# The recurrent layer of a decoder trunk: order of its blocks, form of its gates and gelu, and its first loads

## The chip, the cores and the metric

The kernel runs on one core of a Trainium2 chip. The metric is the device time in microseconds of one execution. The engines are TensorE (PE; PEld is its weight load), VectorE (DVE), ScalarE (ACT), GpSimd (POOL) and SyncE (SP, which issues most DMAs).

## The reference

One recurrent layer is followed by one attention layer, each with a SwiGLU part; 512 tokens, width 1024. The change is in the recurrent layer's mixer alone:

```
proj = rms_norm(x) @ w_in                  # 1024 -> 2048, split in y (first half) and x (second half)
gate = gelu(y, approximate=True)           # tanh form
xc   = causal_depthwise_conv(x)            # 4 taps per channel
r, i = sigmoid(xc @ w_a + b_a), sigmoid(xc @ w_x + b_x)     # 8 diagonal blocks of 128 x 128
log_a = -8 * r * softplus(-lambda);  a = exp(log_a)
u = sqrt(-expm1(2 * log_a)) * i * xc
h_t = a_t * h_(t-1) + u_t                  # scan over the tokens
x = x + (gate * h) @ w_out
```

All inputs and outputs are float32.

## The kernel before

Activations lie transposed: a tile is 128 channels by 512 tokens, the residual stream is eight such tiles `h[0..7]`. A float32 product is made of three matmuls (`mm3`, lines 132 to 136): both operands are split into a rounded high part (`xh`, `wh`) and the rest (`xl`, `wl`), and high*high, high*low and low*high are summed in one PSUM bank. A weight piece is 128 x 1024, one block of 128 output channels; with eight k steps of three matmuls a block takes 24 matmuls of 512 columns.

`Stream` (lines 64 to 125) brings the pieces in order: a DMA on SP's queue into one of two raw buffers (`wr`), then the split: ACT makes `wh` (line 92), and DVE subtracts for `wl` (line 99), or, for pieces of the kind "dma", ACT writes the negated high part (line 95) and a DMA on GpSimd's queue adds the weight to it (line 96). `wh` and `wl` have three buffers each. `get(i)` loads two pieces ahead and splits one ahead. The tile framework orders each engine's instructions from program order, priorities and its own time model, and sets the semaphores.

The start: SP issues the parameters, then the x tiles with the first two weight pieces between them (each in two halves). The split of x makes `xh[k]` on ACT and `xl[k]` on DVE with the norm's gain; the row factor of the norm is multiplied in afterwards, when a block leaves PSUM. The first two blocks run side by side over k (lines 274 to 279). The squares of x (ACT, line 217) are added up on DVE (line 218); `norm_factors` sums over partitions by small matmuls (line 226) and takes the inverse root on DVE; `norm_rows` spreads it with one float32 matmul (line 239), and ACT copies it into `rb` (line 241).

The layer then runs 16 blocks in `lru_order`: five x blocks, then y and x in turn, then the last y blocks. `x_block` (328 to 341) multiplies PSUM by `rb` on DVE, convolves (one ACT, three DVE instructions) and splits the result. `x_gates` (343 to 361) makes two `mm3` products with the split gate weights, in banks "S" (one buffer) and "PT" (two), then two sigmoids and a tanh on ACT. `load_gates` (322 to 326) brings the gate weights on ACT's queue, through the raw buffers `wr`, and splits them. `recur(half)` (363 to 387), once for four blocks, makes exp, square and sqrt on ACT and the scan on DVE. `y_block` (392 to 401) makes the gelu of a square, a tanh (both ACT) and two DVE products; `y_gate` (403 to 405) multiplies with the scanned value and splits into `hgh`, `hgl`. `act_order` orders the groups of ACT functions by edges that make no semaphore. `out_proj` (244 to 256) then runs eight output blocks of 24 matmuls one after the other, and the first SwiGLU part follows. Banks for blocks: four of the tag "mm".

Of the kernel before, what the change touches and what calls it, by code (L numbers as in the profile page):

```python
# [48 lines left out]

class Pool:  # L50
# [13 lines left out]
class Stream:  # L64


    def __init__(self, tc, nc, pool, pieces, ahead_load, ahead_split):
        self.tc, self.nc, self.pool, self.pieces = tc, nc, pool, pieces
        self.al, self.asp = ahead_load, ahead_split
        self.raw, self.parts = {}, {}  # L70
        self.nl = self.ns = self.halved = 0

    def _load(self, i):
# [4 lines left out]
        return [lambda c=c: self.nc.sync.dma_start(r[:, c], ap[:, c]) for c in self._cuts(i, w)]  # L78

    def _cuts(self, i, w):  # L80
        return [slice(0, 512), slice(512, 1024)] if i < self.halved else [slice(0, w)]

    def _split(self, i):
# [6 lines left out]
        def do(c):  # L90
            with self.tc.high_priority():
# [11 lines left out]
    def start(self, n):  # L103

        self.halved = self.nl = self.ns = n
        loads, splits = zip(*[(self._load(i), self._split(i)) for i in range(n)])
        return [[x[j] for x in y] for y in (loads, splits) for j in range(2)]
# [20 lines left out]
def trunk(tc, A, out):  # L128
# [17 lines left out]
    lru_order = [8, 9, 10, 11, 12, 0, 13, 1, 14, 2, 15, 3, 4, 5, 6, 7]  # L146
# [15 lines left out]
    with tc.tile_pool(name="keep", bufs=1) as kp, tc.tile_pool(name="wts", bufs=3) as wp, \  # L162
# [24 lines left out]
        G.memset(ones, 1.0)  # L187
# [16 lines left out]
        def split(src, gain, hi, lo):  # L204
            S.activation(hi, src, AF.Copy, scale=gain)  # L205
            V.scalar_tensor_tensor(lo, src, gain, hi.bitcast(F32), ALU.mult, ALU.subtract)  # L206

# [4 lines left out]
        def squares(k, pool, tag="sq", bufs=1):  # L212
            if k == 0:
                S.activation(ssum, h[0], AF.Square)
            else:
                sq = pool.tile([128, T], F32, name="sq", tag=tag, bufs=bufs)
                S.activation(sq, h[k], AF.Square)
                V.tensor_add(ssum, ssum, sq)
# [15 lines left out]
        def norm_rows(pool, r, tag="sq", bufs=1):  # L234
            dg = pool.tile([128, T], F32, name="dg", tag=tag, bufs=bufs)
            ps = bank("O")
            for n in range(4):
                V.tensor_scalar(dg[:, 128 * n:128 * n + 128], ident, r[:, n:n + 1], None, ALU.mult)
            PE.matmul(ps, ones, dg, start=True, stop=True)
            rb = pool.tile([128, T], F32, name="rb", bufs=1)  # L240
            S.copy(rb, ps)
# [17 lines left out]
        with tc.tile_pool(name="lru", bufs=2) as lp, \  # L259
                tc.tile_pool(name="few", bufs=2) as ls:  # L260
            lp = Pool(lp)
            small = Pool(ls)
            for k in range(KB):
                split(h[k], gain(C_AN, k), xh[k], xl[k])
                run(split_a if k == 0 else split_b if k == 3 else ())
            def in_block(i):
                ps = bank()
                wh, wl = ws.get(i)
                for k in range(KB):
                    c = slice(128 * k, 128 * k + 128)  # L270
                    mm3(ps, (wh[:, c], wl[:, c]), (xh[k], xl[k]), k == 0, k == KB - 1)
                return ps
# [15 lines left out]
            sp8, nsp8 = (small.tile([128, 8], F32, name=n, bufs=1) for n in ("sp8", "nsp8"))  # L288
# [14 lines left out]
            V.tensor_scalar(sp8, lam, -1.0, 0.0, ALU.mult, ALU.max)  # L303
            V.scalar_tensor_tensor(sp8, l3, 2.0, sp8, ALU.mult, ALU.add)
            V.tensor_scalar(sp8, sp8, 8.0, None, ALU.mult)
            V.tensor_scalar(nsp8, sp8, -1.0, None, ALU.mult)
# [7 lines left out]
            gw = [lp.tile([128, 1024], F32R, name=f"gw{i}", bufs=1) for i in range(4)]  # L314
            gated, rate, tau, last_act = [None] * 8, [None] * 4, [None] * 4, [None]

            def act_order(inst):

                tc.add_manual_dep(inst.ins, last_act[0].ins.name, mybir.DependencyInfo(
                    mybir.DependencyClass.NoSync, mybir.DependencyReason.DATA), reason="table order")  # L320

            def load_gates():
                for g in range(2):
# [626 lines left out]
```

## Time and profile before

| | us |
|---|---|
| median of 3 runs | 1257.73 |
| lowest and highest run | 1252.86 and 1258.27 |
| the profiled execution's own time | 1258.03 |
| its span (first to last instruction) | 1256.3 |
| PE, PEld busy | 1222.4 (97%), 1014.8 (81%) |
| DVE, ACT busy | 680.5 (54%), 550.1 (44%) |

A matmul's record is longer than the distance to the next one, since matmuls are pipelined; what one costs is read from the distance between starts. The clock that was granted to TensorE stands in the tables of stretches as a share of 2.4 GHz. The page cuts the span in 40 slices: PE is busy for 7 tenths of the first, 8 of the second and 8 of the fifth, and for 9 tenths or more of nearly all the others.

### The profile page before, as it was taken

What the parts mean: (1) busy time and instruction counts of PE and PEld (TensorE: products, weight loads), DVE (VectorE), ACT (ScalarE), POOL (GpSimd) and SP (SyncE); (2) the same over time, 40 slices, a digit from 0 to 9 for tenths busy, and PEclk for the clock granted to TensorE, in tenths of its full rate; (3) what the DMA queues carried; (4) which work ended last, traced back from release to release, by engine and by line L of the source; (5) the groups of instructions that cost most, each with busy time, mean ns of one, the idle gap of its engine ahead of it and who ended that gap; (6) DMA issues with size and microseconds to landing.
All of it is one profiled execution on the core that took longest, in us unless ns stands there. A gap on an engine that the chain in (4) does not pass through costs nothing.

```text
span 1256.3 us, 14918 instructions
## 1 busy us (share of the span) xinstructions
PE 1222.4 (97%) x5634; PEld 1014.8 (81%) x5634; DVE 680.5 (54%) x1356; ACT 550.1 (44%) x996; POOL 101.9 (8%) x108
## 2 busy tenths in 40 slices
PE   7899899999999999999999999999999999999998
PEld 6678688888888888887878888898888888888887
DVE  7778855444554333377446665765745544552221
ACT  5799533223332222365576766555522323232210
POOL 0100001011111000010111100000011111110000
PEclk9899999999999999999999998599999999999999
DMA  5554222322232333332888664024332233323331
GB/s 190 130 134 118 84 98 87 101 101 93 92 101 97 93 92 95 110 112 86 201 178 186 137 134 101 1 49 99 105 96 91 99 101 101 99 84 103 121 118 46
DMA packets 41257, 133.98 MB, mean 107 GB/s; under 512 B 4960, under 2 KB 7136, under 8 KB 41184
## 3 DMA queue, kind: packets, MB, share of 16 engines
q1 hardware_dynamic: 34416, 110.17, 27.6%
q0 software_dynamic: 5760, 20.97, 10.0%
q10 hardware_dynamic: 1008, 1.88, 0.5%
q8 instruction: 44, 0.72, 0.2%
q14 instruction: 29, 0.24, 0.1%
HBM read 129.86 MB, written 2.10 MB: 105 GB/s over the span
## 4 chain that ended last, share of the span: by engine, by line
PE 79%; ACT 8%; DVE 8%; DMA 3%; issue 1%; SPq 0%; DVEq 0%; ACTq 0%
PE ps L135 23%; PE ps L136 23%; PE ps L134 23%; PE ps L641 3%; PE ps L642 3%; PE ps L643 3%; ACT junk L583 2%; DMA wr<-in_w_q 2%; ACT wh L92 1%; DVE kn L600 1%; ACT wl L95 1%; PE ps L716 1%; DVE wl L99 1%; PE ps L786 1%; DVE gated L386 1%
## 5 line engine op out<-in xcount | busy, mean ns | idle before, releaser
L92 ACT CAST wh<-wr 128x1024 fp32r<-128x1024 f32 (+2 forms) x206 | 210.7, 1024 | 478.7 <-PE ps L135 443.3
L134 PE MATMUL ps<-xh,wh 128*128 128x512 f32 x896 | 353.6, 395 | 11.7 <-ACT xh L205 6.0
L135 PE MATMUL ps<-xl,wh 128*128 128x512 f32 x896 | 351.0, 392 | 0.3 <-DVE xl L206 0.3
L136 PE MATMUL ps<-xh,wl 128*128 128x512 f32 x896 | 351.1, 392 | 0.0
L99 DVE TENSOR_TENSOR wl<-wr,wh 128x1024 fp32r<-128x1024 f32 (+2 forms) x166 | 238.9, 1440 | 152.4 <-ACT wh L92 152.3
L134 PEld LDWEIGHTS ps<-xh,wh 128*128 128x128 f32 x896 | 169.5, 189 | 48.2 <-ACT xh L205 5.9
L135 PEld LDWEIGHTS ps<-xl,wh 128*128 128x128 f32 x896 | 169.6, 189 | 35.9 <-DVE xl L206 1.0
L136 PEld LDWEIGHTS ps<-xh,wl 128*128 128x128 f32 x896 | 169.5, 189 | 35.7 <-issue 0.2
L134 PE MATMUL ps<-gh,wh 128*128 128x512 f32 x352 | 136.9, 389 | 0.0
L135 PE MATMUL ps<-gl,wh 128*128 128x512 f32 x352 | 136.9, 389 | 0.0
L136 PE MATMUL ps<-gh,wl 128*128 128x512 f32 x352 | 136.9, 389 | 0.0
L450 DVE TENSOR_TENSOR u<-ps,rb 128x512 f32<-128x512 f32 x44 | 30.4, 691 | 139.2 <-PE ps L136 139.2
L451 POOL TENSOR_TENSOR u<-u,g 128x512 f32<-128x512 f32 x44 | 59.6, 1354 | 506.7 <-ACT wh L92 362.9
L641 PE MATMUL ps<-wh,xh 128*128 128x512 f32 x224 | 91.2, 407 | 0.0
L643 PE MATMUL ps<-wh,xl 128*128 128x512 f32 x224 | 87.7, 392 | 0.0
L642 PE MATMUL ps<-wl,xh 128*128 128x512 f32 x224 | 87.4, 390 | 0.0
L136 PEld LDWEIGHTS ps<-gh,wl 128*128 128x128 f32 x352 | 66.1, 188 | 13.8
L134 PEld LDWEIGHTS ps<-gh,wh 128*128 128x128 f32 x352 | 66.1, 188 | 13.7
L135 PEld LDWEIGHTS ps<-gl,wh 128*128 128x128 f32 x352 | 66.1, 188 | 13.6
L448 DVE TENSOR_TENSOR g<-ps,rb 128x512 f32<-128x512 f32 x44 | 30.4, 691 | 63.0 <-PE ps L136 62.7
L209 ACT CAST gh<-u 128x512 fp32r<-128x512 f32 x44 | 27.3, 621 | 62.0 <-POOL u L451 62.0
L95 ACT ACTIVATE wl<-wr 128x1024 fp32r<-128x1024 f32 x40 | 42.2, 1056 | 19.0 <-PE ps L642 12.3
(208 smaller groups left out, 1533.8 us busy)
## 6 DMA issues: line engine op xcount, KB each, us to landing
wr<-in_f_in SPq DMA_DIRECT2D x88, 512.0 KB, 3.4
wr<-in_f_out SPq DMA_DIRECT2D x32, 512.0 KB, 3.5
wr<-in_w_q SPq DMA_DIRECT2D x24, 512.0 KB, 6.4
wl<-in_w_q POOLq DMA_DIRECT2D x24, 512.0 KB, 7.0
wr<-in_w_in SPq DMA_DIRECT2D x14, 512.0 KB, 3.7
wr<-in_f_out SPq DMA_DIRECT2D x16, 384.0 KB, 3.1
wr<-in_w_kv SPq DMA_DIRECT2D x12, 512.0 KB, 3.5
wl<-in_w_in POOLq DMA_DIRECT2D x8, 512.0 KB, 7.3
```

Source lines behind the costliest of these rows:

```text
L92: nc.scalar.copy(hi[:, c], r[:, c])
L95: nc.scalar.mul(lo[:, c], r[:, c], -1.0)
L99: eng.tensor_tensor(lo[:, c], r[:, c], hi[:, c].bitcast(F32), ALU.subtract)
L134: PE.matmul(ps, wh, xh, start=first, stop=False)
L135: PE.matmul(ps, wh, xl, start=False, stop=False)
L136: PE.matmul(ps, wl, xh, start=False, stop=last)
L448: V.tensor_tensor(g, pair[0], rb, ALU.mult)
L450: V.tensor_tensor(u, pair[1], rb, ALU.mult)
L451: G.tensor_tensor(u, u, g, ALU.mult)
L641: PE.matmul(ps[t], xh[k][:, r], wh[:, c], start=k == 0, stop=False)
L642: PE.matmul(ps[t], xh[k][:, r], wl[:, c], start=False, stop=False)
L643: PE.matmul(ps[t], xl[k][:, r], wh[:, c], start=False, stop=k == 7)
```

## The change

It does the following in the recurrent layer. The x blocks come first and the y blocks after them. The gate products are single float32 matmuls on unsplit `xc` and unsplit gate weights, which SP loads after the first two blocks straight into their own tiles. The gelu is one ACT function; sqrt works on a tanh of half the argument, so that the square is gone; ACT's functions are ordered in runs. The first two pieces are cut in three, with the first two cuts on ACT's queue; eleven bfloat16 matmuls on a constant tile stand at the start. The norm's small matmuls stand inside the third block and `norm_rows` inside the fourth, with `rb` copied by DVE; a fifth block runs before `rb` is used, in a "PT" bank. The subtractions for piece 3 and 4 are ordered behind the last sum of squares and the last `dg`. Weights are split two ahead in the block loop. The first two output blocks run side by side.

```diff
     def _load(self, i):
-        return [lambda c=c: self.nc.sync.dma_start(r[:, c], ap[:, c]) for c in self._cuts(i, w)]
+        return [lambda c=c, q=q: q.dma_start(r[:, c], ap[:, c]) for c, q in
+                itertools.zip_longest(self._cuts(i, w), self.queues if i < self.cut else (), fillvalue=self.nc.sync)]
...
-        return [slice(0, 512), slice(512, 1024)] if i < self.halved else [slice(0, w)]
+        return [slice(0, 256), slice(256, 512), slice(512, 1024)] if i < self.cut else [slice(0, w)]
...
-                    eng.tensor_tensor(lo[:, c], r[:, c], hi[:, c].bitcast(F32), ALU.subtract)
+                    a = eng.tensor_tensor(lo[:, c], r[:, c], hi[:, c].bitcast(F32), ALU.subtract)
+                    if i in self.hold:
+                        behind(self.tc, a, self.hold[i])
...
-    lru_order = [8, 9, 10, 11, 12, 0, 13, 1, 14, 2, 15, 3, 4, 5, 6, 7]
+    lru_order = [8, 9, 10, 11, 12, 13, 14, 15, 0, 1, 2, 3, 4, 5, 6, 7]
...
-        load_a, load_b, split_a, split_b = ws.start(2)
+        load_a, load_b, load_c, *splits = ws.start(2, nc.scalar, nc.scalar)
         nc.sync.dma_start(par, A["par"])
+        run(load_a + load_b)
         for k in range(KB):
             nc.sync.dma_start(h[k], A["x"][k])
-            run(load_a if k == 0 else load_b if k == 2 else ())
+            run(load_c if k == 3 else ())
...
+            warm = lp.tile([128, T], F32, name="warm", tag="y", bufs=4).bitcast(BF16)[:, :T]
+            V.memset(warm, 1.0)
+            idle = bank("S")
+            for _ in range(11):
+                PE.matmul(idle, warm[:, 0:128], warm, start=True, stop=True)
             for k in range(KB):
-                split(h[k], gain(C_AN, k), xh[k], xl[k])
-                run(split_a if k == 0 else split_b if k == 3 else ())
+                with tc.high_priority():
+                    a = split(h[k], gain(C_AN, k), xh[k], xl[k])
+                    if k:
+                        behind(tc, a, before)
+                    before = a
+                run(splits.pop(0) if k in (0, 1, 3) else ())
...
-            for k in range(KB):
-                squares(k, lp, "q", 2)
-            first.append(in_block(2))
-            r = norm_factors(small)
-            rb = norm_rows(lp, r, "q", 2)
+            gw = [lp.tile([128, 1024], F32, name=f"gw{i}", bufs=1) for i in range(2)]
+            for g in range(2):
+                nc.sync.dma_start(gw[g], A["gates"][g])
+            with tc.high_priority():
+                for k in range(KB):
+                    ws.hold[3] = squares(k, lp, "q", 3)
+            norm = []
+            def soon(fn, *args):
+                with tc.high_priority():
+                    norm.append(fn(*args))
+            first.append(in_block(2, between=lambda: soon(norm_factors, small)))
+            first.append(in_block(3, between=lambda: soon(norm_rows, lp, norm[0], "q", 3, V.tensor_copy, 4)))
+            rb = norm[1]
+            first.append(in_block(4, "PT"))
...
-                ch = lp.tile([128, T], F32R, name="ch")
-                cl = lp.tile([128, T], F32R, name="cl")
-                halve(xc, ch, cl)
-                return b, xc, ch, cl
+                return b, xc
...
-                mm3(pr, (gw[0][:, c], gw[1][:, c]), (ch, cl), True, True)
-                mm3(pi, (gw[2][:, c], gw[3][:, c]), (ch, cl), True, True)
+                PE.matmul(pr, gw[0][:, c], xc, start=True, stop=True)
+                PE.matmul(pi, gw[1][:, c], xc, start=True, stop=True)
...
+            def decays(half):
+                end_run()
+                for b in range(4 * half, 4 * half + 4):
+                    a = rate[b // 2][:, T * (b % 2):T * (b % 2) + T]
+                    done.append(S.activation(a, a, AF.Exp, scale=nsp8[:, b:b + 1]))
+                    act_order(done[-1])
+                end_run()
+                for t in tau[2 * half:2 * half + 2]:
+                    done.append(S.activation(t, t, AF.Sqrt))
+                    act_order(done[-1])
+                end_run()
+            def recur(b):
+                a, t = (x[b // 2][:, T * (b % 2):T * (b % 2) + T] for x in (rate, tau))
+                V.scalar_tensor_tensor(gated[b], a, 1.0, gated[b], ALU.add, ALU.mult)
+                V.tensor_tensor(gated[b], gated[b], t, ALU.mult)
+                V.tensor_tensor_scan(gated[b], a, gated[b], 0.0, ALU.mult, ALU.add)
...
-                t = lp.tile([128, T], F32, name="t", bufs=3)
-                S.activation(t, y, AF.Square, scale=math.sqrt(0.044715))
-                V.scalar_tensor_tensor(t, t, 1.0, y, ALU.add, ALU.mult)
-                S.activation(t, t, AF.Tanh, scale=math.sqrt(2.0 / math.pi))
-                V.scalar_tensor_tensor(t, t, 1.0, y, ALU.add, ALU.mult)
-                return b, t
+                return b, y
+            def y_gate(b, y):
+                g = S.activation(y, y, AF.Gelu_apprx_tanh)
+                act_order(g)
+                V.tensor_tensor(mine(y), mine(y), perm(gated[b]), ALU.mult)
+                halve(y, hgh[b], hgl[b])
...
+            ws.asp = 2
...
-                while xs and xs[0][0] + 2 <= i:
-                    st = xs.pop(0)[1]
-                    x_gates(*st)
-                    if st[0] % 4 == 3:
-                        recur(halves)
-                        halves += 1
-                while ys and ys[0][0] < 4 * halves:
+                for b in decayed[:2]:
+                    recur(decayed.pop(0))
+                while xs and xs[0][0] + (3 if xs[0][0] < 5 else 2) <= i:
+                    b, xc = xs.pop(0)[1]
+                    x_gates(b, xc)
+                    if b % 4 == 3:
+                        decays(b // 4)
+                        decayed += range(b - 3, b + 1)
+                        ready += 1
+                while ys and ready == 2 and ys[0][0] < 8 - len(decayed):
                     y_gate(*ys.pop(0))
...
-            out_proj(p_aout, KB, KB, hgh, hgl, after_a)
+            for ms in ((0, 1), *((m,) for m in range(2, 8))):
+                parts = [ws.get(p_aout + m) for m in ms]
+                first = [bank() for m in ms]
...
```

## Rows read from the trace of the kernel before

**Rows 1.** Busy time by stretch: PE, PEld, DVE, ACT, POOL, granted clock, DMA share, GB/s.

```profile
0.00:171.70 171.70, 153.15 (x635) 121.27 (x636) 133.19 (x208) 121.89 (x167) 8.58 (x23) 0.97 0.47 129
31.90:39.30 7.40, 1.58 (x6) 0.51 (x4) 2.13 (x7) 4.48 (x5) 1.89 (x2) 0.91 0.67 193
38.00:44.60 6.60, 5.32 (x13) 4.17 (x14) 6.23 (x9) 2.44 (x5) 0.95 (x2) 0.50 1.01 213
127.90:130.50 2.60, 0.21 (x2) 0.01 (x1) 2.60 (x4) 0.66 (x2) 0.00 (x0) 0.93 0.16 61
130.50:133.60 3.10, 3.10 (x7) 2.47 (x8) 2.28 (x4) 2.39 (x3) 0.00 (x0) 0.51 0.00 0
171.70:300.00 128.30, 128.30 (x569) 106.00 (x568) 66.49 (x77) 41.27 (x51) 14.18 (x11) 1.00 0.28 95
```

**Rows 2.** PE's timeline, first block of the SwiGLU part: start, us, line, operation.

```profile
171.69 0.39 PE L134 MATMUL ps<-xh,wh 128*128 128x512 f32 x1
...
176.91 0.39 PE L136 MATMUL ps<-xh,wl 128*128 128x512 f32 x1
```

**Rows 3.** PE's waits from 0 to 171.7: us in total, times, longest.

```profile
PE ps L134 <- ACT xh L205: 6.0, 1, 6.0
PE ps L134 <- DVE xp L332: 4.9, 1, 4.9
PE ps L134 <- ACT hgh L209: 3.0, 2, 2.4
PE ps L135 <- DVE cl L210: 1.2, 1, 1.2
```

**Rows 4.** PE's timeline, first two blocks: first, a middle one, and the third block's first.

```profile
5.95 0.79 PE L134 MATMUL ps<-xh,wh 128*128 128x512 f32 x1 [5.95 <-ACT xh L205]
...
10.69 0.40 PE L136 MATMUL ps<-xh,wl 128*128 128x512 f32 x1
...
20.37 0.39 PE L134 MATMUL ps<-xh,wh 128*128 128x512 f32 x1
```

**Rows 5.** PE's timeline after its longest wait.

```profile
39.28 0.80 PE L134 MATMUL ps<-xh,wh 128*128 128x512 f32 x1 [4.91 <-DVE xp L332]
...
44.91 0.40 PE L135 MATMUL ps<-xl,wh 128*128 128x512 f32 x1
```

**Rows 6.** ACT's timeline before that wait's end.

```profile
33.13 1.04 ACT L92 CAST wh<-wr 128x1024 fp32r<-128x1024 f32 x1 [2.27 <-DMA wr<-in_w_in]
...
37.58 0.57 ACT L241 COPY rb<-ps 128x512 f32<-128x512 f32 x1
```

**Rows 7.** ACT's groups from 0 to 171.7: count, busy us, mean ns, idle before.

```profile
L217 ACT ACTIVATE sq<-h 128x512 f32<-128x512 f32 x13 | 8.0, 621 | 1.3 <-DVE ssum L218 1.3
```

**Rows 8.** SP's queue at the start: the last five x tiles.

```profile
4.49 4.33 SPq L185 DMA_DIRECT2D h<-in_x  x5
```

**Rows 9.** PE's timeline around a float32 matmul at full clock.

```profile
183.53 1.02 PE L239 MATMUL ps<-dg,ones 128*128 128x512 f32 x2
...
184.62 0.40 PE L135 MATMUL ps<-xl,wh 128*128 128x512 f32 x1
```

**Rows 10.** DVE's groups from 0 to 171.7.

```profile
L337 DVE SCALAR_TENSOR_TENSOR xc<-xp,par,xc 128x512 f32<-128x512 f32 x24 | 17.6, 747 | 0.9 <-ACT xc L335 0.8
L386 DVE TENSOR_TENSOR_SCAN gated<-rate,gated 128x512 f32<-128x512 f32 x8 | 9.3, 1210 | 0.0
L332 DVE TENSOR_TENSOR xp<-ps,rb 128x512 f32<-128x512 f32 x8 | 8.5, 1078 | 6.8 <-ACT rb L241 5.3 <-PE ps L136 1.6
L361 DVE TENSOR_TENSOR gated<-ig,xc 128x512 f32<-128x512 f32 x8 | 5.5, 688 | 0.1
```

**Rows 11.** ACT's timeline around a table load.

```profile
62.25 0.72 ACT L359 ACTIVATE tau<-rate,sp 128x512 f32<-128x512 f32 x1
62.98 1.28 ACT L370 ACT_TABLE_LOAD   x1
64.27 0.72 ACT L370 ACTIVATE rate<-rate,nsp 128x512 f32<-128x512 f32 x1
```

More of the change, by code (lines that the diff above doesn't have):

```diff
@@ L47, in _three, with behind @@
     return a, b, v - a - b
+def behind(tc, inst, f):
+    tc.add_manual_dep(inst.ins, f.ins.name, mybir.DependencyInfo(
+        mybir.DependencyClass.NoSync, mybir.DependencyReason.DATA), reason="order")
 class Pool:
@@ L98, in do, with start @@
                     eng = nc.gpsimd if kind == "pool" else nc.vector
-                    eng.tensor_tensor(lo[:, c], r[:, c], hi[:, c].bitcast(F32), ALU.subtract)
+                    a = eng.tensor_tensor(lo[:, c], r[:, c], hi[:, c].bitcast(F32), ALU.subtract)
+                    if i in self.hold:
+                        behind(self.tc, a, self.hold[i])
         return [lambda c=c: do(c) for c in self._cuts(i, w)]
-    def start(self, n):
-        self.halved = self.nl = self.ns = n
+    def start(self, n, *queues):
+        self.cut = self.nl = self.ns = n
+        self.queues = queues
         loads, splits = zip(*[(self._load(i), self._split(i)) for i in range(n)])
-        return [[x[j] for x in y] for y in (loads, splits) for j in range(2)]
+        return [[x[j] for x in y] for y in (loads, splits) for j in range(3)]
     def load_to(self, i):
@@ L204, in split @@
         def split(src, gain, hi, lo):
-            S.activation(hi, src, AF.Copy, scale=gain)
+            a = S.activation(hi, src, AF.Copy, scale=gain)
             V.scalar_tensor_tensor(lo, src, gain, hi.bitcast(F32), ALU.mult, ALU.subtract)
+            return a
         def halve(src, hi, lo, eng=None):
@@ L271, in in_block @@
                     mm3(ps, (wh[:, c], wl[:, c]), (xh[k], xl[k]), k == 0, k == KB - 1)
+                    if k == 2 and between:
+                        between()
                 return ps
@@ L348, in x_gates @@
                 sl = slice(T * (b % 2), T * (b % 2) + T)
                 if b % 2 == 0:
[L350 to L351 removed]
+                    rate[b // 2] = lp.tile([128, 2 * T], F32, name="rate", bufs=4)
+                    tau[b // 2] = lp.tile([128, 2 * T], F32, name="tau", bufs=4)
                 r = rate[b // 2][:, sl]
[L353 to L356 removed]
+                act_order(S.activation(r, pr, AF.Sigmoid, bias=gain(C_GA, b)))
@@ L389, in trunk @@
-            hgh = [lp.tile([128, T], F32R, name=f"hgh{k}", bufs=1) for k in range(KB)]
-            hgl = [lp.tile([128, T], F32R, name=f"hgl{k}", bufs=1) for k in range(KB)]
+            def decays(half):
[9 more added lines that the diff above has]
+                end_run()
@@ L392, in y_block @@
+            def recur(b):
[3 more added lines that the diff above has]
+                V.tensor_tensor_scan(gated[b], a, gated[b], 0.0, ALU.mult, ALU.add)
             def y_block(b, i):
-                ps = first.pop(0) if first else in_block(i)
-                y = lp.tile([128, T], F32, name="y")
+                ps = in_block(i)
+                y = lp.tile([128, T], F32, name="y", bufs=4)
```

104 lines of the change are left out of this document (40 added, 64 removed).

## The prediction

> **What bounds the kernel now.** I read the table of stretches first. From 171.7 to 300 us PE is busy for the whole stretch at granted clock 1.00; from 0 to 171.7, which is the recurrent layer, it is not, and the clock there averages 0.97 [rows 1]. So TensorE sets the pace, the layer's own holes are what can be won, and nothing after it is touched by the change. The first SwiGLU matmul starts at 171.69 [rows 2]: that is the layer's end on PE. The reader is to see there also the pitch: from 171.69 to 176.91 lie 23 steps, so a warm matmul of 512 columns costs 0.227 us.
>
> The layer needs (16 + 8) blocks of 24 matmuls and 8 gate steps of 6: 624 x 0.227 = 141.6 us. The norm adds one float32 matmul and some small ones, 1.7 us together (the float32 one is priced below at 0.86, and I give the small ones the same). 171.7 - 143.3 = 28.4 us are lost. PE's waits and timeline say where:
> - 5.95 us before the first matmul [rows 3, 4].
> - The first two blocks run from 5.95 to 20.37 [rows 4], 14.4 us for 48 matmuls that need 10.9: 3.5 lost, about half of it to the slow start, since from 5.95 to 10.69 only nine steps are made.
> - 4.9 us wait for the first `xp` [rows 3]. All four block banks are full, DVE's `xp` waits for `rb`, and on ACT the copy of `rb` at 37.58 stands behind casts whose weights came late, from 33.13 on [rows 6].
> - Restart at half clock: the granted clock is 0.50 from 38.0 to 44.6 [rows 1], and the 13 steps from 39.28 to 44.91 [rows 5] take 5.6 us where 13 x 0.227 = 2.95 would do: 2.7 lost.
> - 3.0 us for `hgh` at the output blocks [rows 3], in the stretch 127.9 to 130.5 above all; then the clock is 0.51 and seven matmuls take 3.1 us [rows 1] for 1.6: 1.5 lost.
> - 1.2 us for `cl` [rows 3].
> These are 22.8 us; the remaining 5.6 are short waits, of weight loads mostly.
>
> **The change part by part.** *Gates.* A float32 matmul is two instructions; from its start at 183.53 to that of the matmul after next at 184.62 lie 1.09 us [rows 9], of which one ordinary step is 0.23: it costs 0.86. So 16 x 0.86 = 13.8 us replace 48 x 0.227 = 10.9: 2.9 us more on PE, on its path. Bounds: if one cost only two plain steps, 0.45, it would be 3.6 less than before; at half clock, 1.72, 16.6 more. I take the row, since it is the same operation and shape. In return eight casts and eight subtractions go from ACT and DVE, and the wait for `cl` (1.2) goes with them. *The gate loads* leave ACT's queue and the raw buffers for SP, behind the loads of pieces 2 and 3; they need no buffer, and nothing reads them before the first gate product, some 15 us later. They move 1 MB, as before.
>
> *First loads.* SP needs 4.33 us to issue the last five x tiles [rows 8]; four weight DMAs now are issued by ACT, which has nothing else at that time but a table load of 1.28 us [rows 11]. I let the first real matmul start at 5.5 instead of 5.95 (from 5.0, if ACT's first cast, half as long, is all that falls away, to 6.5, if the table load now stands behind the four issues). *Warm-up.* Eleven matmuls at half clock, 0.43 us each (5.63/13 [rows 5]), are 4.7 us and end near 5.8 if they start at 1.1: beside the wait for the first loads, so free; if the loads are there sooner, they cost up to 0.5. They take the slow steps away from the real work. In this case nine steps were slow at the start, thirteen after the longest wait and seven after the next [rows 1, 4, 5]. The Trainium skill (TensorE: Matmul & The Clock Gate, "What's actually happening") says likewise that the count of slow matmuls at a start differs from run to run of one kernel, and gives up to 14; then three real ones would be slow, 0.6 us by the pitches above. The sum goes without it.
>
> *Order on ACT at the start.* The casts `xh` now come ahead of the squares (0.62 us each [rows 7]), several of which stood between them. With eight `xh`, the first two blocks are then limited by PE: 10.9 us plus 0.5 that I leave for late x tiles (0 to 2). Saved: 3.0.
>
> *The norm.* The squares follow the casts; SP issues the last x tile by 8.8 [rows 8], so I put the last cast near 13; eight squares take 5 us and end near 18 to 19, while PE reaches the small matmuls (inside the third block, after nine of its matmuls) near 19. Queued behind those on PE is all the rest, so a late sum costs its lateness one to one: I take 1.0 with the later arrival of piece 2 and 3, whose subtraction is held behind the last sum (0 to 4). `norm_rows` stands five us of PE work later, and `rb` is copied by DVE and no longer behind ACT's casts. The fifth block in a "PT" bank gives 5.4 us more cover. So the 4.9 and the 2.7 behind it go. What is late next is DVE, which then has five blocks to evict at 1.08 + 3 x 0.75 + 0.69 = 4.0 us each [rows 10]; PE has a block and two gate steps per 7.2 us, and one bank is free after the first `xp`, so it is hidden.
>
> *Blocks and runs.* Second half: eight scans with their two products, 2.6 us each (1.21 [rows 10] and two at the 0.69 of a product there), leave `recur`; the square, one of three products, and four ACT and DVE steps of the gelu per block are gone. After the last decay PE has six y blocks, 33 us, and the first pair of output blocks needs its last `hgh` only after 42 of 48 matmuls, 9.5 us more. DVE needs for four recurrences 10.4, for eight y blocks 8 x (0.69 + 1.08 + 0.69) = 19.7, for splits about 5: 35 us, under 42. So the 3.0 and the 1.5 behind it go. What stays is ACT's chain at the first decays: three table loads, four exps and two long sqrts, 3.8 + 2.9 + 2.1 = 8.8 us (exp 0.72 [rows 11], the long sqrt put at half as much again), against 7.2 us of PE work before the next product wants the only "S" bank: 1.5 us (0 to 5). At that place the table's price matters. The rows show a tanh that ends at 62.97, a load at 62.98, and the next function at 64.27 [rows 11]: 1.3 in all. The Trainium skill (ScalarE: Activation LUTs, "What ACT_TABLE_LOAD costs") adds a drain, 2.66 us for a switch. By that, the three switches would take 4.1 us longer and the time would come out near 1246, inside the forecast's own case; the rows show no such gap, and I give it 0.05 of that case's 0.60.
>
> *Weights two ahead*: three buffers allow it only as a block's slot comes free, as before; no wait of PE on these weights is among the larger ones. I cost it at nothing (-0.5 to +1).
>
> **Sum.** Work: 576 x 0.227 + 13.8 + 1.7 = 146.3. Lost: 5.5 start, 0.5 first blocks, 1.0 norm, 1.5 decays, and 1.0 for the short waits (of 5.6 before, most of them at split gates and at the output blocks): 9.5. End of the layer 155.8, so 15.9 earlier. From the profiled execution's 1258.0, which is the median of the runs within 0.3, that is 1242. With the least losses (5.0 + 1) it is 1238.5, and with the upper ends of start, first blocks, norm and decays (6.5 + 2 + 4 + 5 + 1) 1251.
>
> **The rivals.**
> - *The tail stays late.* All eight gelus and four recurrences now lie behind the second decays. For it: ACT and DVE are both over 0.7 busy in the layer [rows 1], and the wait for `hgh` was here before. Against: the sum above, 35 under 42. Price: the old 3.0 + 1.5 and about 2.5 of short waits again, 1249.
> - *The eviction stays late*, so the change does not do what it says: the sum of squares or `rb` comes behind other DVE work, the banks fill, and the 4.9 + 2.7 return, with the 3.5 of the first blocks. For it: PE's order is fixed, so nothing passes a late small matmul. Against: DVE copies `rb` itself, and one bank more is there. Loss 20.6, time 1253.
> - *Slower: the single "S" bank.* Each gate product into "S" waits until ACT has made the sigmoid before it, and ACT's functions are now ordered in runs, so a sigmoid can't pass an exp. If PE waits for it at all eight blocks, the price is 8 w. The gain of 15.9 is gone at w = 2.0 us; at w = 2.6, a hole after which rows show half clock [rows 1], it is 20.8 + some cold steps: 1264. Against: the bank was single before, and none of PE's larger waits names a sigmoid [rows 3].
>
> **How the numbers follow.** Forecast (1238 to 1248) 0.60; tail 0.18; late eviction 0.12; slower 0.10. About 0.5% (6.3 us) is what a measurement of this kernel can tell from no change. Faster by more, below 1251.4, are the first two and a small part of the third: 0.79. Within: most of the third, 0.12. Slower by more: 0.09, the last case. The range is 1235 (the least losses, and runs 3 us below the profiled one, as one of three was 5 below) to 1253, which takes in the tail and the late eviction's value.
>
> **What would show it.** Right: PE's first real matmul near 5.5 at a pitch of 0.23, the third block from about 17, no wait on `xp`, granted clock 1.00 from 10 us to the layer's end, float32 gate pairs of 1.7 us, the first SwiGLU matmul near 156, and then the same pitch. Wrong: a wait of PE on ACT's sigmoid, on the small matmuls' input or on `hgh`, a stretch at 0.50, or gate products dearer than 0.86; and anything after 156 that takes longer than before.

## The result and the profile after

| | before | after |
|---|---|---|
| median | 1255.3 (1251.77 to 1258.27, 4 runs) | 1237.92 (1236.72 to 1242.14, 4 runs) |
| profiled execution, its span | 1258.03, 1256.3 | 1236.72, 1234.9 |
| first SwiGLU matmul (the layer's end on PE) | 171.69 [rows 2] | 158.10 |
| from there to the end of the span | 1084.6 | 1076.8 |

The ratio is 0.9886 (0.9856 to 0.9916): faster by 1.1%. 1242 had been forecast. The two profiled executions differ by 21.3 us, and only 13.6 of these lie in the layer that was changed. The other 7.8 lie behind it, in code that is the same; they are looked at below.

What answers to [rows 1] is the busy time by stretch of the changed kernel: PE, PEld, DVE, ACT, POOL (us and instructions), granted clock, DMA share, GB/s.

```profile
0.00:158.10 158.10, 153.03 (x629) 116.43 (x630) 117.43 (x186) 101.30 (x137) 8.58 (x23) 1.00 0.51 140
```

PE is busy for as long as before, 153.0 us against 153.2, but now in 158.1 us instead of 171.7. The clock is 1.00 in the layer, where it was 0.97; the eleven dummy matmuls stand in the 153.0. PE's waits in this stretch (us in total, times, longest) answer to [rows 3]:

```profile
PE ps L283 <- DVE warm L280: 1.5, 1, 1.5
PE ps L148 <- DMA wl<-in_w_in: 1.4, 1, 1.4
PE ps L146 <- ACT xh L218: 0.9, 1, 0.9
PE ps L382 <- ACT rate L389: 0.9, 1, 0.9
PE ps L147 <- DVE xl L219: 0.3, 1, 0.3
```

Of before's waits for `xp`, `hgh` and `cl` none is left in this list. Two have taken their place: 1.4 us for a low weight part that comes by DMA, and 0.9 for a sigmoid. PE's timeline has the places, and answers to [rows 4, 5, 9] (start, duration, line; in brackets the idle time before and what ended it):

```profile
1.46 4.66 PE L283 MATMUL ps<-warm 128*128 128x512 bf16 x11 [1.46 <-DVE warm L280]
5.93 0.73 PE L146 MATMUL ps<-xh,wh 128*128 128x512 f32 x2
...
8.85 0.51 PE L146 MATMUL ps<-xh,wh 128*128 128x512 f32 x1 [0.94 <-ACT xh L218]
9.64 0.50 PE L147 MATMUL ps<-xl,wh 128*128 128x512 f32 x1 [0.28 <-DVE xl L219]
...
21.86 1.02 PE L240 MATMUL ps<-ones,ssum 128*128 128x1 f32 x8
...
27.83 1.02 PE L255 MATMUL ps<-dg,ones 128*128 128x512 f32 x2
...
37.58 1.02 PE L382 MATMUL ps<-xc,gw 128*128 128x512 f32 x2
38.43 1.02 PE L383 MATMUL ps<-xc,gw 128*128 128x512 f32 x2
...
41.77 1.13 PE L382 MATMUL ps<-xc,gw 128*128 128x512 f32 x2 [0.92 <-ACT rate L389]
```

The first real matmul starts at 5.93, as early as before. The sums of the norm at 21.86 and the float32 matmul behind them at 27.83 have no bracket: PE did not wait for them. A float32 gate product costs 38.43 - 37.58 = 0.85 us, as priced.

### The profile page after: what moved, and what is told of

Its sections match the earlier page's. It is cut to its first block, busy times and chain, and to the rows that moved or that the text cites. A ratio compares the mean times of both kernels' runs of the same rounds, so it can differ in the third digit from the quotient of the medians.

```text
span 1234.9 us, 14873 instructions
## 1 busy us (share of the span) xinstructions
PE 1214.6 (98%) x5629; PEld 1003.0 (81%) x5629; DVE 666.6 (54%) x1334; ACT 529.4 (43%) x967; POOL 100.3 (8%) x108
## 4 chain that ended last, share of the span: by engine, by line
PE 85%; ACT 6%; DVE 6%; DMA 2%; issue 1%; SPq 1%; ACTq 0%
PE ps L147 24%; PE ps L148 24%; PE ps L146 24%; PE ps L673 3%; PE ps L675 3%; PE ps L674 3%; ACT junk L615 2%; DVE kn L632 1%; DMA wr<-in_w_q 1%; ACT wh L100 1%; PE ps L748 1%; ACT wl L103 1%; DMA wl<-in_w_in 1%; PE ps L818 1%; PE ps L382 1%
## 5 line engine op out<-in xcount | busy, mean ns | idle before, releaser
L100 ACT CAST wh<-wr 128x1024 fp32r<-128x1024 f32 (+3 forms) x208 | 211.2, 1016 | 498.6 <-PE ps L147 450.3
L107 DVE TENSOR_TENSOR wl<-wr,wh 128x1024 fp32r<-128x1024 f32 (+2 forms) x168 | 241.4, 1438 | 152.4 <-ACT wh L100 152.2
L147 PEld LDWEIGHTS ps<-gl,wh 128*128 128x128 f32 x352 | 66.1, 188 | 13.6
```

The costliest lines, as they stand in the source:

```text
L100: nc.scalar.copy(hi[:, c], r[:, c])
L107: a = eng.tensor_tensor(lo[:, c], r[:, c], hi[:, c].bitcast(F32), ALU.subtract)
L147: PE.matmul(ps, wh, xl, start=False, stop=False)
```

## The experiments

Each edit is planned anew as a whole, so the order on an engine can shift with it; where that decided, it is told. The end of the layer on PE is the sharpest measure: four profiles whose instructions up to there have the same order (the changed kernel twice, e4 and e6 below) give 158.10, 159.99, 157.66 and 156.40. The latest of them lost some 2 us to a longer wait and slow steps in the first two blocks, and the earliest had no wait for the low weight part. Every other kernel has one profile. Differences under about 4 us are therefore read from the waits and steps that make them, not from the sum.

| run | layer's end | median (range) | ratio to before, interval |
|---|---|---|---|
| b1 gates alone | 165.40 | 1247.05 (1240.89 to 1249.32) | 0.9948 (0.9929 to 0.9968) |
| b2 gates and order | 163.80 | 1246.10 (1236.55 to 1251.53) | 0.9948 (0.9924 to 0.9972) |
| e1 no warm-up | 161.20 | 1239.89 (1236.79 to 1244.89) | 0.9887 (0.9851 to 0.9923) |
| e3 old norm | 157.79 | 1237.91 (1235.91 to 1241.52) | 0.9873 (0.9836 to 0.9909) |
| e4 one ahead | 157.66 | 1238.96 (1236.58 to 1244.22) | 0.9881 (0.9847 to 0.9916) |
| e7 old gelu | 158.69 | 1239.43 (1237.69 to 1239.77) | 0.9898 (0.9881 to 0.9915) |
| e2b split gates | 154.71 | 1235.57 (1233.40 to 1236.84) | 0.9868 (0.9849 to 0.9888) |
| e5 x first | 156.83 | 1236.09 (1235.76 to 1237.80) | 0.9855 (0.9827 to 0.9882) |
| e8 split and x | 155.32 | 1236.97 (1235.05 to 1240.36) | 0.9868 (0.9833 to 0.9904) |
| e6 fill | 156.40 | 1238.92 (1238.05 to 1240.39) | 0.9876 (0.9848 to 0.9904) |
| f1 after again | 159.99 | 1238.48 (1235.87 to 1242.69) | 0.9888 (0.9870 to 0.9906) |
| f2 split again | 155.40 | 1235.82 (1233.72 to 1239.27) | 0.9870 (0.9851 to 0.9888) |

**b1: the kernel before with the gates' edit alone.**

```diff
-                    r = wp.tile([128, 1024], F32, name="gr", tag="wr", bufs=2)
-                    S.dma_start(r, A["gates"][g])
-                    halve(r, gw[2 * g], gw[2 * g + 1])
+                    nc.sync.dma_start(gw[g], A["gates"][g])
...
-                mm3(pr, (gw[0][:, c], gw[1][:, c]), (ch, cl), True, True)
+                PE.matmul(pr, gw[0][:, c], xc, start=True, stop=True)
...
```

> The kernel before with one edit: the gate weights are loaded by SP as float32 into tiles of their own and used as they are, the conv outputs are not cut; order of blocks, gelu, norm, first loads and weights as before. Theory (the stall at the first eviction came from the gate weights standing in the two raw buffers, which made the weight casts behind them late): the wait of 4.9 for the first xp and the 2.7 of slow steps go, and the 1.2 for the cut conv output, against 2.8 more on PE for 16 float32 products: layer end 171.7 - 7.6 - 1.2 + 2.8 = 165.7. Rival (the stall came from elsewhere and only the products change): 171.7 - 1.2 + 2.8 = 173.3, the wait on xp of some 4 to 5 us still there.

The layer ended at 165.40, 0.3 from the theory. Its three largest waits on PE:

```profile
PE ps L134 <- ACT xh L205: 6.1, 1, 6.1
PE ps L134 <- ACT hgh L209: 2.7, 2, 2.5
PE ps L341 <- DVE xc L335: 2.6, 2, 2.3
```

The wait for `xp` is gone with the gates' edit alone, with the old norm and the old first loads in place. The tail's wait for `hgh` is there as in [rows 3], and one of 2.3 for a conv output has come forward.

**b2: the same, and all x blocks ahead of the y blocks.**

```diff
-    lru_order = [8, 9, 10, 11, 12, 0, 13, 1, 14, 2, 15, 3, 4, 5, 6, 7]
+    lru_order = [8, 9, 10, 11, 12, 13, 14, 15, 0, 1, 2, 3, 4, 5, 6, 7]
...
-                gated[b] = lp.tile([128, T], F32, name="gated", bufs=6)
+                gated[b] = lp.tile([128, T], F32, name="gated", bufs=8)
...
```

> The kernel before with two edits: the float32 gates as in the run beside it, and all eight x blocks ahead of the y blocks (eight gated tiles instead of six); gelu, norm, first loads as before. Theory (the order sets the tail: the last recurrences and gelus get more cover): the wait for hgh of 3.0 and the 1.5 of slow steps go, layer end 4 to 5 us ahead of that of the gates alone, near 161. Rival (with all gelus in their old form behind the second decays, ACT and DVE are later than before): the wait for hgh stays or grows, layer end equal to that of the gates alone or later.

163.80, only 1.6 ahead of b1: between the two, and less than profiles of one kernel differ by. PE's waits:

```profile
PE ps L134 <- ACT xh L205: 5.9, 1, 5.9
PE ps L341 <- DVE xc L335: 2.5, 2, 2.3
PE ps L134 <- ACT hgh L209: 1.6, 1, 1.6
PE ps L134 <- ACT wh L92: 1.3, 1, 1.3
PE ps L135 <- DVE hgl L210: 0.6, 1, 0.6
```

At the output blocks 2.7 became 1.6 + 0.6. The order alone does not give the tail enough cover.

**e7: the changed kernel with the old gelu.** The run leaves out a factor of one half that the kernel before has in its square roots.

```diff
+                t = lp.tile([128, T], F32, name="ig")
+                S.activation(t, y, AF.Square, scale=math.sqrt(0.044715))
+                V.scalar_tensor_tensor(t, t, 1.0, y, ALU.add, ALU.mult)
+                g = S.activation(t, t, AF.Tanh, scale=math.sqrt(2.0 / math.pi))
+                act_order(g)
+                V.scalar_tensor_tensor(y, t, 1.0, y, ALU.add, ALU.mult)
...
-                g = S.activation(y, y, AF.Gelu_apprx_tanh)
-                act_order(g)
```

> The changed kernel with the gelu of the kernel before (square on ACT, two products on DVE around it, tanh on ACT, a last product), all else as changed. Theory (the order with all eight x blocks first gives enough cover, so that the tail had no need of the shorter gelu): no wait of PE on hgh over 0.5 us at the output blocks, layer end within 0.5 of 158.1. Rival (the one-function gelu is what took the tail's stall away): the wait for hgh of 2 to 3 us returns, with slow steps behind it, and the layer ends at 161 to 163.

158.69. The sum looks like the theory, but the timeline of PE at the output blocks is the rival's, at half its size:

```profile
124.04 0.51 PE L146 MATMUL ps<-hgh,wh 128*128 128x512 f32 x1 [1.37 <-ACT hgh L223]
124.77 0.50 PE L147 MATMUL ps<-hgl,wh 128*128 128x512 f32 x1 [0.22 <-DVE hgl L224]
```

The sum hides it because this execution did not have the 1.4 us for the low weight part. Against the fill run (e6), which did not have it either and reached the norm's float32 matmul at 27.58 against 27.57 here, the old gelu costs 158.69 - 156.40 = 2.3 us; up to 124 us PE's starts in the two stay within 0.2 us of each other. So the order needs the new gelu beside it: b2 and e7 have the one without the other, and PE waits 2.2 and 1.6 us there. The new gelu in the old order was not run, nor was the pairing of the first two output blocks, which e7 has and b2 has not.

**e3: the changed kernel with the old norm** (squares not hurried, factors behind the third block, `rb` copied by ACT, no fifth block in a "PT" bank).

```diff
...
-            first.append(in_block(2, between=lambda: soon(norm_factors, small)))
-            first.append(in_block(3, between=lambda: soon(norm_rows, lp, norm[0], "q", 3, V.tensor_copy, 4)))
-            rb = norm[1]
-            first.append(in_block(4, "PT"))
+            first.append(in_block(2))
+            r = norm_factors(small)
+            rb = norm_rows(lp, r, "q", 3)
```

> The changed kernel with the norm as before: squares without priority, its matmuls after the third block, rb copied by ACT, no held subtractions, no fifth block ahead. Theory of the prediction (the norm's place and ACT's copy made the long wait): 4.9 us of wait on xp and 2.7 of half clock come back, the end near 165.7. Rival (the wait came from the gate weights in the raw buffers, which made the casts ahead of the copy late): the end within 2 us of 158.1 and no wait on xp over 1 us.

157.79, and PE's two largest waits behind the start are these:

```profile
PE ps L148 <- DMA wl<-in_w_in: 1.4, 1, 1.4
PE ps L146 <- ACT xh L218: 1.1, 1, 1.1
```

No wait on `xp`. Beside b1 this settles the cause of the 4.9 + 2.7 of before: the gate weights in the two raw buffers made the weight casts behind them late, and ACT's copy of `rb` stood behind the casts. The kernel before shows the buffers at work, in DVE's timeline and in the waits of SP's queue:

```profile
28.46 1.23 DVE L210 TENSOR_TENSOR gw<-gr,gw 128x1024 fp32r<-128x1024 f32 x1
SPq L78 <- DMA gr<-in_gates: 6.8, 1, 6.8
SPq L78 <- DVE gw L210: 2.0, 1, 2.0
```

SP stands for 6.8 us and issues its next weight load at 29.71, when the subtraction of the first gate weight has ended (28.46 + 1.23 = 29.69); the load behind it follows the second subtraction, at 32.15. In b1 the two are issued at 22.01 and 24.48. That the gate weights also left ACT's queue was not varied by itself; their casts are not the cause, since e2b below has them back and no wait on `xp`. The new place of the norm has nothing left to win that the waits or the layer's end show.

**e1: without the eleven dummy matmuls** (the tile, its memset and the loop over `PE.matmul(idle, ...)` removed).

```diff
-            for _ in range(11):
-                PE.matmul(idle, warm[:, 0:128], warm, start=True, stop=True)
```

> The changed kernel without the eleven matmuls on the constant tile. Read at the layer's end on PE, the first SwiGLU matmul (158.1 us in the changed kernel, 171.7 before). Theory (the warm-up takes the slow steps away from real work): nine slow steps at 0.43 instead of 0.227 come back, the end moves to 159.1 to 160.0. Rival (the first blocks wait for the loads anyway, 2.3 us of it, so slow steps are hidden in these waits): the end stays within 0.5 of 158.1. A gain (end before 157.6) would mean that the warm-up holds the first real matmul back.

161.20, later than either said. PE's timeline shows why:

```profile
6.00 0.80 PE L146 MATMUL ps<-xh,wh 128*128 128x512 f32 x1 [6.00 <-ACT xh L218]
...
9.95 0.40 PE L148 MATMUL ps<-xh,wl 128*128 128x512 f32 x1
...
19.04 0.39 PE L146 MATMUL ps<-xh,wh 128*128 128x512 f32 x1
...
21.45 1.02 PE L240 MATMUL ps<-ones,ssum 128*128 128x1 f32 x8 [1.34 <-DVE ssum L232]
...
23.56 0.57 PE L146 MATMUL ps<-xh,wh 128*128 128x512 f32 x1
...
26.91 0.45 PE L148 MATMUL ps<-xh,wl 128*128 128x512 f32 x1
```

Steps at half clock are there from 6.00 to 9.95, and yet PE is no later at the third block: 19.04, where the changed kernel has 19.14 (18.87, 18.88 and 21.27 in the other profiles of its order). They lie in time that the changed kernel spends waiting for the second x tile. The 3 us arise at 21.45. In the new plan the norm's small matmuls stand behind four matmuls of the third block, in the changed kernel behind eleven; PE came too early, waited 1.34 for the sum of squares, and eight slow steps followed (23.56 to 26.91), 3.35 us where 8 x 0.227 = 1.8 would do: with the wait 2.9 of the 3.1 us. So the loss is that of a moved instruction, and the warm-up by itself is worth next to nothing here. That PE would have lost nothing with the old order was not run.

**e4: weights split one ahead, as before.**

```diff
-            ws.asp = 2
```

> The changed kernel with weights split one ahead throughout. The order of every engine's instructions and their waits come out the same as with two ahead, so that part of the change should do nothing: end of the layer at 158.1 within 0.3. It serves as a second look at the changed kernel. Theory on the rest of the span (7.8 us less after the layer's end, though nothing there was changed: the length of the half-clock stretch in the attention differs from execution to execution): times fall apart by 4 to 6 us with the mean clock, near 1237 at 0.99 and near 1242 at 0.985. Rival (the shorter layer shifts the attention so that it always loses less): all times within 1.5 us of 1237.

Every engine has the same instructions in the same order with or without this line; 157.66, 0.1 outside what was said, is the changed kernel once more. Its times go with the mean clock, as the theory on the rest of the span has it: 1236.58 and 1238.33 us at 0.990, 1239.58 at 0.986, 1244.22 at 0.985.

**e2b and f2: the changed kernel with split gate products.** The float32 weights land in tiles of `tau`, one cast and two subtractions cut each of them, and the low parts stand in tiles that the output blocks fill only later: with tiles of their own for all parts (e2) the layer would need 151 KB per partition, where 124 are free.

```diff
...
+                ch, cl = hgh[b % 4], hgl[b % 4]
+                halve(xc, ch, cl)
...
-                PE.matmul(pr, gw[0][:, c], xc, start=True, stop=True)
+                mm3(pr, (gw[0][:, c], gwl[0][b // 4][:, lc]), (ch, cl), True, True)
...
```

> The changed kernel, but the gate products are split again: both gate weights are loaded where the changed kernel loads them, cut once into two parts by one cast on ACT and two subtractions on DVE each, each conv output is cut again (one cast, one subtraction per block), and each product is three matmuls. Theory (the float32 matmul costs PE what its row says, 0.855 us against 0.68, and nothing else depends on it): 16 x (0.855 - 0.68) = 2.8 us less on PE, so the layer ends on PE near 158.1 - 2.8 = 155.3 and the time is some 3 us shorter. Rival (the casts and subtractions that the float32 form saves matter): 10 casts and 12 subtractions return to ACT and DVE, a wait for the cut conv output or for a sigmoid of over 2 us in all appears, and the layer ends at 158 or later.

154.71, 3.4 us earlier. The float32 products cost what their row said, 2.8 of it; the other 0.6 are waits, 3.0 us of them behind the start here and 3.6 in the changed kernel. The casts that come back are not free, though. PE waits at a gate product for the bank that a sigmoid has to empty:

```profile
79.52 0.50 PE L146 MATMUL ps<-hgh,gw 128*128 128x512 f32 x1 [1.49 <-ACT rate L399]
```

On ACT the cast of a conv output waits 1.67 us for DVE and starts at 77.65, and the sigmoid stands behind it, from 78.80. The changed kernel has no wait there; the profiles of f2 and e8, with the same casts, have 1.47 and 1.49. The split form gains by 2.8 and gives some 1.5 back. So that part of the change gained by where the weights were put, and lost by how they were multiplied. Both kernels ran again side by side, as f1 and f2:

> The changed kernel itself, run again beside the version with split gates on one chip, so that the two are compared directly. Both theories of the float32 products: layer end 158.1 within 0.4 (157.7 in the run in which only an order was named that did not change), median 1236.5 to 1239, with single runs up to 1244 where the granted clock is lower.

> The changed kernel with split gate products, run again: layer end 154.7 within 0.6. Theory (what the layer's end gains stays to the end of the program): median 2.5 to 3.5 us below that of the changed kernel beside it. Rival (the attention's half-clock stretches take it back or hide it): within 1 us of it.

Layer ends 159.99 and 155.40, medians 1238.48 and 1235.82: 2.7 us apart, as the theory has it. Both layer ends are later than was said (158.1 within 0.4, 154.7 within 0.6), and of the 4.6 us between them 2.3 lie in the first two blocks, where f1 had slow steps: its third block starts at 21.27, that of f2 at 18.94. The intervals of the two ratios to before overlap (0.9870 to 0.9906 and 0.9851 to 0.9888), so by time alone the split form is likely, not surely, the faster; by the layer's end it is: 154.71 and 155.40 against 156.40 to 159.99 in four profiles of the changed kernel's order.

**e5 and e8: the second x tile's cast ahead of the second weight casts**, in the changed kernel and in e2b.

```diff
...
                 run(splits.pop(0) if k in (0, 1, 3) else ())
+                if k == 1:
+                    for f in ws.casts[-2:]:
+                        behind(tc, f, before)
...
```

> The changed kernel with one more order: the two casts of the second weight tile's first quarters stand behind the cast of the second x tile on ACT, so that they no longer hold it up while their load is under way. Theory (the 2.3 us lost in the first two blocks come from the second x cast waiting behind a weight cast whose load is late): the second x cast starts 1 us or more earlier, the wait of 0.9 us for it on PE goes, and the layer ends near 157 (156.5 to 157.5). Rival (PE only waits for the next thing, the weight cast itself, or the x tile has not landed either): the wait appears at another name and the layer ends within 0.4 of 158.1.

In the changed kernel ACT's timeline at the start is this, and PE waits 0.9 at 8.85:

```profile
5.16 0.72 ACT L218 ACTIVATE xh<-h,par 128x512 fp32r<-128x512 f32 x1
7.77 0.40 ACT L100 CAST wh<-wr 128x256 fp32r<-128x256 f32 x1 [1.90 <-DMA wr<-in_w_in]
8.08 0.72 ACT L218 ACTIVATE xh<-h,par 128x512 fp32r<-128x512 f32 x1
...
```

ACT holds its order: at 7.77 it waits 1.90 for a weight load, and the x tile's cast stands behind. With the edit:

```profile
6.48 0.72 ACT L219 ACTIVATE xh<-h,par 128x512 fp32r<-128x512 f32 x1
7.11 0.39 ACT L101 CAST wh<-wr 128x256 fp32r<-128x256 f32 x1
7.68 0.41 ACT L101 CAST wh<-wr 128x256 fp32r<-128x256 f32 x1 [0.18 <-DMA wr<-in_w_in]
```

The cast of the second x tile (6.48) is 1.6 us earlier, PE's wait at 8.85 is gone, and the layer ended at 156.83, within the theory's bounds. That end alone would show little, since the fill run ended at 156.40 without the edit; but the third block starts at 17.64, where the four profiles of the changed kernel's order have 18.87 at the earliest. A part of this may be the weight load, which had landed by 7.11 instead of 7.77; and PE's order in the first two blocks shifted with the edit.

> Two edits to the changed kernel together: gate products split in three again (layer end 154.7 alone) and the second x cast ahead of the second weight casts. Theory (the two gains lie at different places and add): layer end 154.7 minus what the second edit gives alone, 153.5 to 154; median near 1234. Rival (the early blocks then wait for the evictions instead): layer end 154.7 within 0.4.

155.32, outside both expectations and nearer to the rival: the two gains did not add. The third block starts at 18.36, only 0.4 and 0.6 us before that of e2b and f2. In this execution the x tile itself was late (its cast at 7.18, after 0.72 us for its load), so how much the order gives depends on which load lands first.

**e6: dummy matmuls in the attention's later part**, four ahead of each set of transposes and ten of 256 columns ahead of each set of value products.

```diff
...
+    def spin(out, n):
+        for _ in range(n if quiet[0] else 0):
+            PE.matmul(out, busy[:, 0:128], busy[:, 0:out.shape[-1]], start=True, stop=True)
...
+        spin(pt, 4)
...
+        spin(po[:, 128 * (p - 1):128 * (p + 1)], 10)
...
```

> The changed kernel with matmuls that compute nothing of the result put into the attention's later part, where there is no other work to fill PE: before each set of transposes 4 of 512 columns, before each set of value products 10 of 256 columns, both into banks that the work behind them overwrites. Theory (the 7.8 us by which the two profiled executions differ behind the layer, in code that is the same, are half clock after short holes in this part): the granted clock from 700 to 900 us is 0.99 to 1.00 and the runs lie closer together, with a median 5 to 10 us below that of the changed kernel if the holes were long enough to take the fillers, and 0 to 5 above where the fillers push real work back. Rival (the difference has another cause): the clock there stays near 0.94, or it is 1.00 and the runs still spread over 5 us or more.

The question was where the 7.8 us behind the layer come from. The busy table of the kernel before, for the 200 us that begin 540 after the layer's end, with three stretches of its later attention:

```profile
711.69:911.69 200.00, 192.74 (x1077) 170.09 (x1076) 134.63 (x436) 113.67 (x262) 12.53 (x14) 0.91 0.36 84
...
791.69:801.69 10.00, 9.09 (x43) 8.34 (x43) 8.86 (x24) 5.25 (x11) 0.00 (x0) 0.53 0.01 2
801.69:811.69 10.00, 10.00 (x50) 10.00 (x49) 4.73 (x19) 2.88 (x11) 0.00 (x0) 0.50 0.00 1
811.69:821.69 10.00, 10.00 (x45) 9.06 (x45) 6.00 (x23) 4.46 (x14) 0.00 (x0) 0.60 0.00 0
```

and the same part of the changed kernel:

```profile
698.10:898.10 200.00, 191.43 (x1101) 167.88 (x1101) 136.60 (x431) 114.38 (x262) 13.83 (x15) 0.94 0.36 85
...
768.10:778.10 10.00, 8.01 (x38) 7.33 (x36) 10.00 (x40) 6.34 (x13) 0.00 (x0) 0.50 0.00 0
...
788.10:798.10 10.00, 10.00 (x44) 9.39 (x45) 5.62 (x22) 4.16 (x13) 0.00 (x0) 0.52 0.00 1
```

In the one PE runs near 1.2 GHz (clock 0.50 to 0.60) for three stretches of 10 us, and in part of the one before them (0.66); in the other for two (0.50 and 0.52), and in part of the one between them (0.84). Over the 200 us the clock is 0.91 and 0.94; 0.03 of 200 us is 6 us' worth of matmuls, by estimate. With the fillers it is 0.97, neither the theory's 0.99 nor the rival's 0.94, and the mean clock of the four executions 0.994 to 0.997, against 0.985 to 0.990; but their median, 1238.92, is no better: the fillers take back what the clock gives. The spread shrank to 2.3 us, which four runs don't prove, since e5's four lie within 2.0. So the clock is shown to differ, and by size it could be most of the 7.8. The other profiles bear this out in part. From the layer's end to the end of the span b2 takes 1084.3 us at 0.91, like before with 1084.6; but f1 and e2b, at 0.95, take 1079.4 and 1080.3, longer than the 1076.8 of the changed kernel at 0.94. Some 3 us between executions have another cause, which stays open. The clock differs between executions of one kernel: of the runs of before beside these experiments, the four at mean clock 0.980 average 1257.4 and the eight at 0.987 1251.8.

## Why the prediction was right, and where it was not

**The sum.** Forecast: the layer ends at 155.8, 15.9 earlier. Measured: 158.10 in the first profile, 13.6 earlier, and 158.0 in the mean of the four; before has one profile, so the 13.6 is good to some 2 us, an estimate from the scatter of those four. The layer gained less than was forecast, and yet the median of 1237.92 lies under 1242. That is luck: the 7.8 us behind the layer have no term in the forecast but "runs 3 us below the profiled one". The sum started from the profiled execution of before, at a mean clock of 0.981, and its executions near that clock are its longest. Over all its runs (the first four, e4 and f1) the changed kernel has a median of 1238.3, and the 44 of before beside the experiments one of 1253.1: 14.8 us, of which the layer is 13.7. One reading of the prediction is off by one: from 5.95 to 10.69 lie eight steps, not nine, and 0.8 us of that stretch is a wait; no term of the sum hangs on it.

**The losses, 11.8 instead of 9.5:**

| term | forecast | measured |
|---|---|---|
| start | 5.5 | 5.93 |
| first two blocks | 0.5 | 2.3 (5.93 to 19.14 for 10.9 of work) |
| norm | 1.0 | 0 |
| decays | 1.5 | 0 |
| short waits and the rest | 1.0 | 3.6, of which 1.4 the low weight part, 0.9 the first sigmoid, 1.3 in no listed wait |

- *First two blocks.* The step that failed is "are then limited by PE". It costed late x tiles (0 to 2), not a weight cast that waits for its load on ACT ahead of the next x cast. e5 shows this to be the place: with the order turned round the third block starts at least 1.2 us earlier.
- *Norm and decays.* The norm's sum came in time and the decays held PE up nowhere. The single "S" bank, the mechanism of the slower rival and a sign of being wrong by the prediction's own list, shows at one product instead of eight: 0.92 us ahead of the second pair of gate products at 41.77. ACT's timeline:

```profile
38.69 1.03 ACT L100 CAST wh<-wr 128x1024 fp32r<-128x1024 f32 x1
39.74 1.28 ACT L389 ACT_TABLE_LOAD   x1
41.03 0.69 ACT L389 ACTIVATE rate<-ps,par 128x512 f32<-128x512 f32 x1
```

A weight cast and the load of the sigmoid's table precede the first sigmoid, and the second product waits for its bank. The load starts at 39.74 and the sigmoid at 41.03, 1.3 us as in [rows 11]; the 2.66 that the Trainium skill (ScalarE: Activation LUTs, "What ACT_TABLE_LOAD costs") gives for a switch is not seen here either.
- *The low weight part.* It was issued at 101.3, in the fill run at 101.1, but took longer to land here (the tile's instructions, and its load's us to landing):

```profile
L104 POOL DMA_DIRECT2D wl<-in_w_in x1: 860/860/860, 101.3 to 101.3; - x1
DMA to landing us min/median/max: 8.1/8.1/8.1
```

In the fill run the same load took 6.6 us, and the wait is not there. Eight low parts of the layer take this way, before as after. "Weights two ahead", costed at nothing, changed no order (e4), so it did not help here.

**What the gains are from.** *Eviction:* 4.9 + 2.7 went, as forecast, and for the cause that was read from [rows 6], late casts. The remedy was named wrongly: it credits the norm's new place, DVE's copy and the fifth bank, and e3 and b1 show that it was the gate loads out of the raw buffers, which the text lists without a price. *Tail:* 3.0 + 1.5 went; the text gave that to order and gelu in one sum, and b2 and e7 show that the order alone does not do it; what the gelu alone would do was not run. *Gates:* +2.9 on PE was right (2.8 in e2b). The return for it, priced at the 1.2 of `cl`, shows in e2b as 1.5 at a sigmoid and 0.2 at a low part. *Warm-up:* "They take the slow steps away" is true of the changed kernel's first profile, and worth next to nothing there, since without them those steps lie in a wait for loads (e1); in f1 slow steps came back behind the wait for the second x tile.

**By parts**, from the layer's ends: gates' own loads and float32 products -6.3 (b1), order -1.6 (b2), and the rest of the change -5.7; each is the difference of two single profiles, and that of the order is within their scatter. Of the last, about 2.3 is the gelu (e7). Who has the remaining 3.4 is not shown: the look-ahead of three blocks for the gate products and the first loads, which were not run alone, are the likeliest, since b2's wait of 2.3 for a conv output and its 1.3 for a weight cast at the start are gone after.

## What to carry to other kernels

When a load is to go through a buffer that other work needs next, ask first what that buffer's next user is: here tiles of their own for 1 MB of weights were worth more than any other part that was run, and the float32 products that came with them gave 3 us of it back. Slow steps and warm-up are worth only what lies on the path: look whether the next wait would swallow them. And an experiment that takes an instruction away can move others; compare the orders before crediting the difference to what was removed.

## What was not expected of the hardware

Holes of the same length on PE were followed by half clock in one run and not in another. After the wait of 1.41 us at 109.46 in the changed kernel the clock stayed at 1.00; after one of 1.38 and another of 0.28 in f1 it fell (granted clock in the column before the last two):

```profile
109.00:116.00 7.00, 6.54 (x29) 5.42 (x30) 5.19 (x8) 4.26 (x6) 0.00 (x0) 1.00 0.47 151
```

The row of f1:

```profile
9.40:14.20 4.80, 4.46 (x11) 3.31 (x12) 4.50 (x8) 4.80 (x10) 0.00 (x0) 0.64 0.92 298
```

After a wait of 2.34 us in b1 it fell as well,

```profile
78.50:86.00 7.50, 7.48 (x22) 5.08 (x23) 6.89 (x10) 7.39 (x10) 0.95 (x2) 0.77 0.65 145
```

and after one of 2.27 at the gate product of the next block in b2 it did not:

```profile
76.80:84.00 7.20, 7.12 (x24) 4.60 (x25) 6.73 (x10) 6.75 (x11) 0.00 (x0) 1.00 0.45 93
```

In b1 itself a wait of 2.52 at the output blocks (125.83) left it at 1.00. The prediction had counted slow steps behind the longer holes of the kernel before, and with its slower rival. By these rows a hole's length alone does not settle whether they follow; a forecast must hold both cases, some 1.5 us apart (eight slow steps in e1).
